# Low parts of the up projection's weights by an accumulating DMA, in a two-layer decoder trunk in split float32

## The chip, the cores and the metric

The kernel runs on one core of a Trainium2 chip. The metric is device time in microseconds (us) of one execution. Before the change it was 2156.09 us in the median of three runs (2155.92 to 2156.14). The five engines of the core work side by side and wait for each other by semaphores: TensorE (PE; its weight loads are PEld), VectorE (DVE), ScalarE (ACT), GpSimd (POOL) and SyncE (SP). In this kernel SP does nothing but issue DMAs.

## The reference

The program is a trunk of two pre-norm residual layers over 1024 tokens of width 1024. The first layer mixes tokens by a convolution and an mLSTM, the second by gated linear attention; behind each mixer stands a SwiGLU feed-forward block of hidden width 2816, and a norm closes the trunk. What the change touches is in the feed-forward blocks:

```python
def swiglu(h, w1, w3, w2):
    return (jax.nn.silu(h @ w1) * (h @ w3)) @ w2

for l in range(DEPTH):
    ...
    h = rmsnorm(x, ffn_norm_g[l])
    x = x + swiglu(h, ffn_w1[l], ffn_w3[l], ffn_w2[l])
```

Everything is float32.

## The kernel before, in words

**Split float32.** PE multiplies operands of a rounded type, float32r. To keep float32's precision every operand x is cut into a high part, x rounded, and a low part, x minus the high part. A product is then three matmuls (lines 168 to 170, in `mm3`): low part of the left operand with the high part of the right, high with low, high with high. In `split` (line 141) ScalarE copies x into the high tile, which rounds it, and VectorE subtracts that from x into the low tile. Tiles named `wH` and `wL` hold the two parts of weights, `hH` and `hL` those of activations.

**The up projection** (`ffn_up`) computes h @ w1 and h @ w3 with seven products instead of eight, in Winograd's form: tokens and the depth are halved, hidden columns are halved too, and each step p of 11 takes 128 columns of each half. Its weights come as four tiles of 128 x 1024, a11, a12, a21, a22 (`load`, line 1021), each with w1 and w3 side by side. The seven products of a step are named after their operands: B11 uses a11, B21 a12, T4 a22, and T1 = a21 + a22, T2 = T1 - a11, T3 = a11 - a21, B22 = a12 - T2 use sums that VectorE makes into tiles `S` (`s`, line 1028). For each product `v(x)` makes the high and low tile of its weights, and `prod` runs 24 matmuls: 12 into a PSUM bank of the kind `mm` (for w1), 12 into one of the kind `sm` (for w3). VectorE and ScalarE take the banks' results apart (lines 1075 and 1082, `c` tiles), and a new tile of the result goes to memory.

**Order of steps.** For p = 0 to 4 (`LEAD = 5`) the products B11 and B21 are made first, ten products in a row, while the norm and the operands of the second half of the tokens are still being made. Then the other five products of p = 0 to 4 follow: T2, T3, T1, T4, B22. From p = 5 on all seven of a step come together, B11 and B21 first. There are 7 x 11 = 77 products per layer, 154 in all.

**Buffers.** `wH` and `wL` have three buffers each, shared with the other weights of the program: the parts of a product can be made when the product three before it has ended. The tiles a11 and a12 (`raw` of the stage's pool) have four buffers, a21 and a22 (`raw` of the program's pool) two, `S` three. A buffer is given again when all its readers are done.

**Order on the engines.** A scheduler of the framework places the program's instructions when it is built. It goes by its own estimate of each instruction's time and by priorities (`high_priority`; here `UOFF = 300`, which lets the preparation of weights run ahead), and each engine then executes its list in the order that was fixed so. An instruction that waits holds up everything behind it on its engine; SP and POOL hold their DMAs in the same way. Norms: `rstd_half` squares eight tiles on ScalarE (line 197), adds them on VectorE (199) and sums over partitions with a matmul on PE (202).

In the profile the products of the up projection are the rows of lines 168 to 170 with `wL` and `wH` of 128 x 1024; the lines of `split` show as L141.

Of the kernel before, what the change touches and what calls it, by code (L numbers as in the profile page):

```python
# [11 lines left out]
AF = mybir.ActivationFunctionType  # L12
ALU = mybir.AluOpType
# [60 lines left out]
def trunk_kernel(ctx, tc, xT, cols, gate_b0, ev_vo0, ev_u, ev_cw, ev_out, od_v0, od_u, od_out, gate_w2, fin_row,  # L74
                 w13, w2, out, xsp, rowd, ud, zd, ad, md):
    nc = tc.nc
    PE, ACT, DVE, POOL, SP = nc.tensor, nc.scalar, nc.vector, nc.gpsimd, nc.sync
# [10 lines left out]
    def nm(s):  # L88
        uid[0] += 1
        return f"{s}_{uid[0]}"  # L90
# [48 lines left out]
    def split(dst, src, lo, after=None):  # L139

        ins = ACT.activation(dst[0], src, AF.Copy), lo.tensor_tensor(out=dst[1], in0=src, in1=dst[0], op=ALU.subtract)  # L141
        for i, a in zip(ins, after or ()):
            behind(i, a)
        return ins[1]

    def behind(ins, other):

        tc.add_manual_dep(ins.ins, other.ins.name, mybir.DependencyInfo(mybir.DependencyClass.NoSync, mybir.DependencyReason.DATA))
# [854 lines left out]
    def ffn_up(l, hv, fp):  # L1003
# [10 lines left out]
        def prep(p):  # L1014
            with tc.high_priority(offset=UOFF):
                def load(q):
                    if q < 2:
                        t = fp.tile([P, 1024], F32, tag="raw", name=nm("raw"), bufs=4)
                    else:
                        t = wp.tile([P, 1088], F32, tag="raw", name=nm("raw"), bufs=2)[:, :1024]  # L1020
                    SP.dma_start(t, w13[l, p, q])
                    return t

                a11, a12 = load(0), load(1)

                def s(x, y, op):
                    t = fp.tile([P, 1024], F32, tag="S", name=nm("S"), bufs=3)
                    DVE.tensor_tensor(out=t, in0=x, in1=y, op=op)
                    return t

                def v(x):
                    hi = wp.tile([P, 1088], F32R, tag="wH", name=nm("wH"))[:, :1024]
                    low = wp.tile([P, 1088], F32R, tag="wL", name=nm("wL"))[:, :1024]
                    split((hi, low), x, DVE)
                    return hi, low

                vs = {"B11": lambda: v(a11), "B21": lambda: v(a12), "T4": lambda: v(ss["a22"])}
                ss = {}

                def sums():  # L1040
                    a21, a22 = load(2), load(3)
                    ss["a22"] = a22
                    ss["T1"] = s(a21, a22, ALU.add)
                    ss["T2"] = s(ss["T1"], a11, ALU.subtract)
                    ss["T3"] = s(a11, a21, ALU.subtract)

                def get(name):
                    with tc.high_priority(offset=UOFF):
                        if name in vs:
                            return vs[name]()  # L1050
                        if not ss:
                            sums()
                        if name == "B22":
                            ss["B22"] = s(a12, ss["T2"], ALU.subtract)
                        return v(ss[name])
                return get
# [491 lines left out]
```

## Time and profile before

| What | before |
|---|---|
| median of three runs | 2156.09 us |
| span of the profiled execution, from first to last instruction | 2155.3 us |
| PE busy / its weight loads | 2145.3 / 1823.8 us |
| VectorE busy | 1541.7 us |
| ScalarE busy | 868.6 us |
| GpSimd busy | 22.9 us |
| data moved by DMA | 279.02 MB, mean 129 GB/s |
| first layer's up projection | from 444 us to 864 us of the span |
| second layer's up projection | from 1516 us to 1935 us of the span |

All times of a stage are in us from the start of the span. The profiled execution is one execution; its span lies 0.8 us below the median of the timed runs. "Idle before" in a row is the time for which the engine stood still before an instruction, and the arrow names what ended it. A name without a number stands for all buffers of that kind.

### The profile page before, as it was taken

Reading aid. Unit: us, or ns where it says so; the run is one execution under the profiler, and the core shown is the slowest. Engines: PE = TensorE matmul, PEld = TensorE weight load, DVE = VectorE, ACT = ScalarE, POOL = GpSimd, SP = SyncE. Lnnn points to the kernel's source line nnn. Section 1 sums busy time; section 2 is a strip of 40 time slices with the busy share of each in tenths; the row PEclk is TensorE's granted clock in tenths of the full one; section 3 lists DMA queues with packets and bytes.
Section 4 is the critical chain, followed back from the end, with each engine's and each line's share of the span. In section 5 each row is a group of like instructions: output and inputs, shape, how many; then the busy total and the mean of one; then the engine's idle time right before and its main releaser. Section 6 shows DMA issues by size and latency. Waiting matters only on the chain.

```text
span 2155.3 us, 28752 instructions
## 1 busy us (share of the span) xinstructions
PE 2145.3 (100%) x10750; PEld 1823.8 (85%) x10750; DVE 1541.7 (72%) x2586; ACT 868.6 (40%) x1426; POOL 22.9 (1%) x56
## 2 busy tenths in 40 slices
PE   9999999999999999999999999999999999999998
PEld 8889988888888888888889989888888888888887
DVE  7555788787776666867877746587877766668687
ACT  6302337453222322444564534355522222234554
POOL 0000000000000000000020000000000000000000
PEclk9999999999999999999999999999999999999999
DMA  4233453654432336645321011155544433265344
GB/s 159 89 123 109 141 140 116 213 187 167 166 135 95 106 107 210 203 118 167 109 71 40 21 49 30 40 160 173 193 149 166 137 95 112 97 244 172 97 128 147
DMA packets 138219, 279.02 MB, mean 129 GB/s; under 512 B 22304, under 2 KB 35488, under 8 KB 138080
## 3 DMA queue, kind: packets, MB, share of 16 engines
q1 hardware_dynamic: 137808, 276.92, 39.6%
q8 instruction: 85, 1.39, 0.3%
q14 instruction: 54, 0.44, 0.1%
q10 hardware_dynamic: 272, 0.26, 0.0%
HBM read 210.51 MB, written 66.62 MB: 129 GB/s over the span
## 4 chain that ended last, share of the span: by engine, by line
PE 99%; DVE 1%; DMA 0%; ACT 0%; issue 0%; SPq 0%; DVEq 0%; ACTq 0%
PE mm L168 21%; PE mm L169 21%; PE mm L170 21%; PE sm L170 9%; PE sm L168 9%; PE sm L169 9%; PE sm L405 2%; PE sm L869 1%; PE sm L888 1%; PE sm L887 1%; PE sm L890 1%; PE sm L618 0%; PE sm L842 0%; PE sm L917 0%; PE sm L620 0%; PE sm L585 0%
## 5 line engine op out<-in xcount | busy, mean ns | idle before, releaser
L169 PE MATMUL mm<-hL,wH 128*128 128x512 f32 x1420 | 557.5, 393 | 0.0
L170 PE MATMUL mm<-hH,wH 128*128 128x512 f32 x1420 | 554.7, 391 | 0.0
L168 PE MATMUL mm<-hH,wL 128*128 128x512 f32 x1420 | 520.2, 392 | 1.3 <-DVE wL L162 1.0
L168 PEld LDWEIGHTS mm<-hH,wL 128*128 128x128 f32 x1420 | 267.0, 188 | 57.5 <-ACT hH L332 1.4
L170 PEld LDWEIGHTS mm<-hH,wH 128*128 128x128 f32 x1420 | 267.2, 188 | 55.1 <-issue 0.2
L169 PEld LDWEIGHTS mm<-hL,wH 128*128 128x128 f32 x1420 | 267.1, 188 | 54.8 <-DVE hL L333 0.5
L169 PE MATMUL sm<-hL,wH 128*128 128x512 f32 x616 | 240.1, 390 | 0.0
L170 PE MATMUL sm<-hH,wH 128*128 128x512 f32 x616 | 239.7, 389 | 0.0
L168 PE MATMUL sm<-hH,wL 128*128 128x512 f32 x616 | 209.0, 390 | 0.0
L141 ACT ACTIVATE wH<-S 128x1024 fp32r<-128x1024 f32 x88 | 93.2, 1060 | 212.4 <-PE sm L170 212.3
L141 ACT ACTIVATE wH<-q 128x512 fp32r<-128x512 f32 x143 | 90.4, 632 | 178.5 <-PE mm L170 101.1
L141 DVE TENSOR_TENSOR wL<-q,wH 128x512 fp32r<-128x512 f32 x143 | 98.6, 689 | 72.2 <-ACT wH L141 71.8
L168 PE MATMUL mm<-wH,hL 128*128 128x256 f32 (+2 forms) x512 | 145.3, 287 | 0.6 <-DVE xy L1271 0.6
L169 PE MATMUL mm<-wL,hH 128*128 128x256 f32 (+2 forms) x512 | 145.6, 286 | 0.0
L170 PE MATMUL mm<-wH,hH 128*128 128x256 f32 (+2 forms) x512 | 145.5, 286 | 0.0
L169 PEld LDWEIGHTS sm<-hL,wH 128*128 128x128 f32 x616 | 115.7, 188 | 24.7 <-issue 0.7
L168 PEld LDWEIGHTS sm<-hH,wL 128*128 128x128 f32 x616 | 115.6, 188 | 24.4 <-PE mm L170 0.5
L170 PEld LDWEIGHTS sm<-hH,wH 128*128 128x128 f32 x616 | 115.6, 188 | 24.2 <-issue 0.2
L141 DVE TENSOR_TENSOR wL<-S,wH 128x1024 fp32r<-128x1024 f32 x88 | 107.4, 1221 | 23.9 <-ACT wH L141 23.9
L1075 DVE TENSOR_TENSOR c<-sm,c 128x512 f32<-128x512 f32 x110 | 75.6, 687 | 67.6 <-PE sm L170 67.6
L161 ACT ACTIVATE wH<-raw 128x1024 fp32r<-128x1024 f32 (+2 forms) x77 | 81.4, 1057 | 96.6 <-PE mm L170 66.7
L162 DVE TENSOR_TENSOR wL<-raw,wH 128x1024 fp32r<-128x1024 f32 (+2 forms) x77 | 94.1, 1222 | 35.4 <-ACT wH L161 35.4
(332 smaller groups left out, 3688.3 us busy)
## 6 DMA issues: line engine op xcount, KB each, us to landing
raw<-in_w SPq DMA_DIRECT2D x108, 512.0 KB
mdT<-c SPq DMA_DIRECT2D x88, 256.0 KB
m<-mdT SPq DMA_DIRECT2D x88, 256.0 KB
mdB<-c SPq DMA_DIRECT2D x66, 256.0 KB
q<-in_w SPq DMA_DIRECT2D x60, 256.0 KB
m<-mdB SPq DMA_DIRECT2D x55, 256.0 KB
xsp<-xy SPq DMA_DIRECT2D x48, 256.0 KB
raw<-in_od_u SPq DMA_DIRECT2D x22, 512.0 KB
```

The costliest lines, as they stand in the source:

```text
L141: ins = ACT.activation(dst[0], src, AF.Copy), lo.tensor_tensor(out=dst[1], in0=src, in1=dst[0], op=ALU.subtract)
L161: first = ACT.activation(hi, raw, AF.Copy)
L162: cuts = lo.tensor_tensor(out=low, in0=raw, in1=hi, op=ALU.subtract)
L168: return (PE.matmul(o, lt[1], rt[0], start=start and not on, stop=False, skip_group_check=on), PE.matmul(o, lt[0], rt[1], start=False, sto ...
L169: PE.matmul(o, lt[0], rt[1], start=False, stop=False, skip_group_check=on),
L170: PE.matmul(o, lt[0], rt[0], start=False, stop=stop, skip_group_check=on))
L405: PE.matmul(o, w[:, m * P:(m + 1) * P], raw[:, e, m:m + NT], start=m == 0, stop=m == SH)
L869: PE.matmul(lb[:, j * P:(j + 1) * P], X[:, 2 * j * P:(2 * j + 1) * P], X[:, (2 * j + 1) * P:(2 * j + 2) * P], start=True, stop=True)
L887: PE.matmul(db[:, cc, :], kw[:, cs], v[:, c, :], start=True, stop=True)
L888: PE.matmul(ob[:, cc, :], A[:, cs], v[:, c, :], start=True, stop=st is None)
L890: PE.matmul(ob[:, cc, :], qt[:, cs], st, start=False, stop=True)
L1075: DVE.tensor_tensor(out=out, in0=a, in1=b, op=ALU.add)
```

## The change

The three lines below replace one call of `split` in `v`. ScalarE now writes both tiles from x: the high one as before, and the low one as the negative of the same rounded value. Then an accumulating DMA, issued on GpSimd's queue, reads x and adds it to the low tile, from SBUF to SBUF, so that the tile holds x minus its rounded value as before. The source is a `raw` tile (three of seven products) or an `S` tile (four of seven). VectorE has no part in it any more. All other weights and activations are split as before.

```diff
                 def v(x):
                     hi = wp.tile([P, 1088], F32R, tag="wH", name=nm("wH"))[:, :1024]
                     low = wp.tile([P, 1088], F32R, tag="wL", name=nm("wL"))[:, :1024]
-                    split((hi, low), x, DVE)
+                    ACT.activation(hi, x, AF.Copy)
+                    ACT.activation(low, x, AF.Copy, scale=-1.0)
+                    POOL.dma_start(low, x, accum_op=ALU.add)
                     return hi, low
```

Lines behind the edit are two higher in the changed kernel; its two copies stand on lines 1034 and 1035, its DMA on 1036.

The scheduler places the instructions anew. Three places show how.

First, TensorE at the start of the first layer's up projection. `wL_760` and `wH_759` are the weights of B11 of p = 0, `wL_771` and `wH_770` those of B11 of p = 1; L202 is the norm's sum for the second half of the tokens. Before:

```order
L168 MATMUL mm_757_4326<-hH3_638_3863,wL_760_4329 128x512
L169 MATMUL mm_757_4326<-hL3_639_3864,wH_759_4328 128x512
L170 MATMUL mm_757_4326<-hH3_638_3863,wH_759_4328 128x512
L168 MATMUL mm_768_4398<-hH0_632_3848,wL_771_4401 128x512
L169 MATMUL mm_768_4398<-hL0_633_3849,wH_770_4400 128x512
```

And with the change:

```order
L168 MATMUL mm_757_4326<-hH3_638_3863,wL_760_4329 128x512
L169 MATMUL mm_757_4326<-hL3_639_3864,wH_759_4328 128x512
L170 MATMUL mm_757_4326<-hH3_638_3863,wH_759_4328 128x512
L202 MATMUL sm_696_4194<-s_688_4171,ones_d_87 128x512
L168 MATMUL sm_758_4327<-hH0_632_3848,wL_760_4329 128x512
L169 MATMUL sm_758_4327<-hL0_633_3849,wH_759_4328 128x512
```

Before, L202 stood behind 12 more matmuls, those of B11 of p = 1 into its first bank; now it stands directly behind the first 12 of the stage.

Second, TensorE in the row of ten products, where the weights of B11 of p = 3 (`wL_793`) take the buffer of those of B21 of p = 1 (`wL_775`). The rows are with the change; left out are 11 more of the same product, `wL_786` (B21 of p = 2).

```order
L168 MATMUL sm_769_4401<-hH7_646_3883,wL_775_4438 128x512
L169 MATMUL sm_769_4401<-hL7_647_3884,wH_774_4437 128x512
L170 MATMUL sm_769_4401<-hH7_646_3883,wH_774_4437 128x512
L170 MATMUL sm_780_4475<-hH3_638_3863,wH_781_4476 128x512
L168 MATMUL mm_779_4474<-hH4_640_3868,wL_786_4512 128x512
...
L168 MATMUL mm_790_4548<-hH0_632_3848,wL_793_4551 128x512
L168 MATMUL sm_791_4549<-hH0_632_3848,wL_793_4551 128x512
```

Between the last matmul that reads `wL_775` and the first that reads `wL_793` stand 13 matmuls; before, it was 36. By the same count 19 matmuls stand between the weights of B11 of p = 2 and the last on the buffer that they take, and 24 for B11 of p = 4.

Third, ScalarE in the regular part, around T2, T3 and T1 of p = 1 (tiles `wH_854`, `wH_858`, `wH_864`) and T4 of p = 1 (`wL_871`), whose source is a22. Before:

```order
L1130 ACTIVATE c_833_4796<-c_833_4796 128x512
L141 ACTIVATE wH_854_4902<-S_852_4898 128x1024
L1134 ACTIVATE c_827_4762<-c_827_4762 128x512
L141 ACTIVATE wH_858_4934<-S_853_4900 128x1024
L1138 ACTIVATE c_812_4686<-c_812_4686 128x512
L141 ACTIVATE wH_864_4968<-S_851_4896 128x1024
```

And with the change:

```order
L1132 ACTIVATE c_833_4809<-c_833_4809 128x512
L1035 ACTIVATE wL_855_4918<-S_852_4913 128x1024
L1034 ACTIVATE wH_854_4917<-S_852_4913 128x1024
L1136 ACTIVATE c_827_4774<-c_827_4774 128x512
L1035 ACTIVATE wL_859_4951<-S_853_4915 128x1024
L1034 ACTIVATE wH_858_4950<-S_853_4915 128x1024
L1140 ACTIVATE c_812_4696<-c_812_4696 128x512
L1035 ACTIVATE wL_865_4986<-S_851_4911 128x1024
L1034 ACTIVATE wH_864_4985<-S_851_4911 128x1024
L1035 ACTIVATE wL_871_5024<-raw_850_4909 128x1024
```

Of each pair the scheduler puts the copy for the low tile first, so that the DMA can be issued while the high tile is copied. On GpSimd the 77 DMAs of a layer stand in the order of the products, each behind a wait for its low tile's copy.

## The prediction

> **What bounds the kernel now.** First the page's top, its DMA queues and its chain of work:
>
> ```profile
> span 2155.3 us, 28752 instructions
> PE 2145.3 (100%) x10750; PEld 1823.8 (85%) x10750; DVE 1541.7 (72%) x2586; ACT 868.6 (40%) x1426; POOL 22.9 (1%) x56
> q1 hardware_dynamic: 137808, 276.92, 39.6%
> PE 99%; DVE 1%; DMA 0%; ACT 0%; issue 0%; SPq 0%; DVEq 0%; ACTq 0%
> ```
>
> TensorE idles 10 us of 2155.3; VectorE is on 1% of the chain. Then the busy times of the stretches in which the two up projections run:
>
> ```profile
> 435.00:500.00 65.00, 65.00 (x286) 53.37 (x285) 52.77 (x72) 33.79 (x51) 0.00 (x0) 1.00 0.56 187
> 500.00:640.00 140.00, 140.00 (x620) 115.95 (x619) 106.31 (x130) 37.13 (x42) 0.00 (x0) 1.00 0.44 151
> 640.00:865.00 225.00, 225.00 (x994) 186.38 (x993) 145.12 (x175) 65.07 (x80) 0.00 (x0) 1.00 0.40 134
> 1507.00:1570.00 63.00, 63.00 (x277) 51.68 (x276) 52.60 (x72) 33.76 (x50) 0.00 (x0) 1.00 0.57 191
> 1710.00:1935.00 225.00, 225.00 (x994) 186.38 (x993) 146.08 (x176) 65.05 (x80) 0.00 (x0) 1.00 0.39 131
> ```
>
> The columns after the stretch are its length, then busy time of PE, PEld, DVE, ACT, POOL, granted clock, DMA share and GB/s. PE is busy for every microsecond of these stretches, at the full clock: 140/620 = 0.226 us per matmul, so a product of 24 matmuls takes 5.42 us. The edited code has nothing to win here; it can only make PE wait.
>
> **What is removed and added.**
>
> ```profile
> L141 DVE TENSOR_TENSOR wL<-S,wH 128x1024 fp32r<-128x1024 f32 x44 | 53.7, 1220 | 11.9 <-ACT wH L141 11.9
> L141 DVE TENSOR_TENSOR wL<-raw,wH 128x1024 fp32r<-128x1024 f32 x33 | 40.2, 1219 | 2.5 <-ACT wH L141 2.5
> L141 ACT ACTIVATE wH<-S 128x1024 fp32r<-128x1024 f32 x44 | 46.6, 1059 | 105.9 <-PE sm L170 105.9
> ```
>
> These groups are those of the first layer's up projection; both layers have 154 low parts. VectorE loses 2 x (53.7 + 40.2) = 188 us, all under a busy PE: worth nothing. ScalarE gains 154 x 1.06 = 163 us; in 500 to 640 it worked 37 of 140 us, so the 26 further copies (28 us) fit. GpSimd gains 154 transfers of 512 KB; it has no other work in these stretches (POOL 0.00).
>
> What changes is when a low part is ready. Its buffer comes free when the product three before it ends; then come the copy on ScalarE and, in place of one subtraction, a time **L** from the end of that copy until PE knows the accumulation landed. The copy of wH runs beside it and is no part of L.
>
> **The price of L.** No accumulating or GpSimd transfer stands in the trace. The nearest row is the 512 KB load of this stage, from its issue on SP to the sum that waits for it:
>
> ```profile
> 507.45 0.33 SPq L1021 DMA_DIRECT2D raw<-in_w  x1
> 511.42 1.23 DVE L1028 TENSOR_TENSOR S<-raw,raw 128x1024 f32<-128x1024 f32 x1 [2.95 <-DMA raw<-in_w]
> 534.71 0.33 SPq L1021 DMA_DIRECT2D raw<-in_w  x1
> 539.13 1.23 DVE L1028 TENSOR_TENSOR S<-raw,raw 128x1024 f32<-128x1024 f32 x1 [3.47 <-DMA raw<-in_w]
> 0.41 0.10 POOL L1521 MEMSET const-uint8-127<- 128x1 uint8 x1
> 1092.53 2.84 POOL L724 TENSOR_SCALAR_AFFINE_SELECT mft<-mft 128x128 f32<-128x128 f32 x1
> ```
>
> That is 4.0 and 4.4 us, mean 4.2. The accumulation reads two tiles: by the q1 row 276.92 MB took 39.6% of the span, so 0.524 MB takes 1.62 us of all sixteen engines, and I add one such reading. GpSimd's issue lies between its shortest and longest instruction, 0.1 and 2.8; I take 0.8, nearer the short end like SP's 0.33, which adds 0.5. L = 4.2 + 1.6 + 0.5 = 6.3 us. Lowest: 0.33 + 1.62 = 2.0, if only the bytes of one reading count. Highest: 2.8 + 4.1 + 2 x 1.62 = 10.1, with the longest issue and each of two reads and the write paid separately.
>
> [...] I stay with 6.3, because the loads of this stage took over 4 us for one reading.
>
> **Where L is longer than its window.** From the last matmul on the buffer to the copy, and from the copy on, around the T2 product of p = 1 and 2:
>
> ```profile
> 531.82 0.39 PE L170 MATMUL sm<-T2H,wH 128*128 128x512 f32 x1
> 532.30 1.06 ACT L141 ACTIVATE wH<-raw 128x1024 fp32r<-128x1024 f32 x1 [4.37 <-PE sm L170]
> 533.46 1.22 DVE L141 TENSOR_TENSOR wL<-raw,wH 128x1024 fp32r<-128x1024 f32 x1
> 540.27 0.68 DVE L1075 TENSOR_TENSOR c<-sm,c 128x512 f32<-128x512 f32 x1
> 542.01 1.22 DVE L1028 TENSOR_TENSOR S<-S,raw 128x1024 f32<-128x1024 f32 x1
> 553.81 0.39 PE L168 MATMUL mm<-T2H,wL 128*128 128x512 f32 x1
> ```
>
> The copy starts some 0.5 us after the product's last matmul and takes 1.06, so L may be the matmuls in between x 0.226 less 1.6. Two whole products lie between in the regular order: 10.8 - 1.6 = 9.2 us, nothing lost at 6.3. But the order of the changed kernel has closer places:
> - Lead, per layer: low part of B11 of p = 2 with 19 matmuls in between (2.7 us allowed), B11 of p = 3 with 13 (1.3), B11 of p = 4 with 24 (3.8), T2 of p = 0 with 36 (6.5), T1 of p = 0 with 31 (5.4). At 6.3: 3.6 + 5.0 + 2.5 + 0 + 0.9 = 12.0.
> - p = 5 to 10, 12 in all: again T2 with 36 and T1 with 31: 0 + 0.9, times 12 = 10.8.
> - T2 of p = 1 to 4, eight in all: the load of a22 (L1021) waits for the buffer that T4's accumulation of p - 1 reads, and SP's queue stands behind it. From 532.30: copy 1.06, L, load until the sum 4.42, sums 2.96 (1.14 from 539.13 to the add at 540.27, 0.6 for that add, 1.22 for the second sum; the low part between them goes), copy 1.06, L; due at 553.81, 21.51 later. 21.51 - 9.50 = 12.0 for 2L, so L may be 6.0; at 6.3 each loses 0.6, together 4.8.
>
> The stall at a stage's start comes from two moves on PE and ACT:
>
> ```profile
> 444.07 0.39 PE L168 MATMUL mm<-hH,wL 128*128 128x512 f32 x1
> 446.79 0.40 PE L168 MATMUL mm<-hH,wL 128*128 128x512 f32 x1
> 449.55 1.02 PE L202 MATMUL sm<-s,ones_d 128*128 128x512 f32 x2
> 444.32 1.06 ACT L141 ACTIVATE wH<-raw 128x1024 fp32r<-128x1024 f32 x1 [3.85 <-issue]
> 445.29 0.61 ACT L197 ACTIVATE t<-xy 128x512 f32<-128x512 f32 x1
> 446.56 0.69 DVE L199 TENSOR_TENSOR s<-s,t 128x512 f32<-128x512 f32 x1
> ```
>
> The norm's matmul L202 now stands behind one group of 12 instead of two, due at 446.8; ahead of the last square ScalarE makes two copies: 444.32 + 2 x 0.97 + 0.61 + 0.69 = 447.6. With the hand-overs PE waits about 1 us, once per layer, and everything behind L202 with it.
>
> Sum: 2 x (12.0 + 1.0) + 10.8 + 4.8 = 41.6 us on the span of 2155.3. The runs' median lies 0.8 above that span (2156.09), so 2197.7, **2198 us**. In general, with brackets below zero left out: S(L) = 2 x [1 + (L-2.7) + (L-1.3) + (L-3.8) + (L-6.5) + (L-5.4)] + 12 x [(L-6.5) + (L-5.4)] + 16 x (L-6.0). S(4) = 10, S(5) = 16, S(7.5) = 99, S(9) = 174.
>
> **The rivals.** 0.2% (4.3 us) is about what a measurement of this kernel can tell from no change.
> - *Hidden* (not slower): an accumulation that lands within 2.4 us of its copy pays at most B11 of p = 3 and the norm: 2 x (1 + 1.1) = 4.2, and at 2.0 3.4 us, 2159. For it: 1.62 us of bytes, SBUF at both ends. Against: single loads take 4.0. Chance 0.08. A true gain has only the 10 us of PE idle, nearly none of them here: 0.03.
> - *Short* (L of 2.4 to 5): the lead alone pays, 4 to 16 us, 2166 at L = 4. Chance 0.2.
> - *One accumulation per product can't be kept*: the DMA engines are 0.40 to 0.56 busy already, 0.44 over a stage's 430 us. In 5.42 us there is room for 0.56 x 5.42 = 3.0 us. Two passes (3.24) overfill it, and if L grows by queueing to 9 the time is 2155.3 + 0.8 + 174 = 2330. Three passes (4.86) make the stage DMA-bound: 0.44 + 4.86/5.42 = 1.34, a third more of 2 x 430 us, 2448. The same price per product falls due if GpSimd's own issue passes 5.42 us. For it: the shares of DMA. Against: packets of an add may overlap their reads. Chance 0.24.
> - [...] Chance 0.08. [...]
>
> **How the numbers follow.** Likeliest is the forecast's case, L of 5 to 7.5: 0.37, 2172 to 2255. The range holds eight tenths: below it the hidden case and a part of the short one, above it the heavier half of the third: 2162 to 2380. Faster 0.03; within 0.2% 0.08; slower 0.89.
>
> **What would show it.** In the new profile the two stretches get longer and the rest stays; PE idles before L168 with a DMA from the GpSimd queue as releaser, mostly in the first 60 us of each stage and at T1 and T2 later; DVE falls by 188 us, ACT rises by 163. Idle before every product, or a DMA share near 1, would show the third rival. No idle on L168 would prove L wrong. Idle of PE on banks, behind sums that wait for S, would be a cause that I have left out.

## The result and the profile after

The changed kernel takes 2274.95 us in the median of three runs (2272.27 to 2281.43) against 2156.09 (2155.92 to 2156.14) before: a ratio of 1.0557, 95% interval 1.0535 to 1.058. It is 119 us slower; the forecast had 42 us, in a range that ended at 2380.

From the page of the changed kernel, its top and the DMA queue of the accumulations (packets, MB, share of the sixteen engines):

```profile
span 2272.9 us, 29372 instructions
PE 2184.1 (96%) x10750; PEld 1838.8 (81%) x10750; DVE 1365.9 (60%) x2432; ACT 1006.1 (44%) x1580; POOL 154.2 (7%) x210
q0 software_dynamic: 22176, 80.75, 18.6%
```

The span grew by 117.6 us with the same 10750 matmuls. Two parts make this up, and both can be read here: PE's busy time grew by 38.8 us (2145.3 to 2184.1), and its idle time by 78.8 us (10.0 to 88.8). VectorE's busy time fell by 176 us and ScalarE's rose by 138; neither is near its limit. The 154 accumulations are queue q0.

The stretches of the first layer's up projection (length; busy time of PE, PEld, DVE, ACT, POOL; granted clock; DMA share; GB/s):

```profile
435.00:500.00 65.00, 62.32 (x262) 49.70 (x261) 38.74 (x59) 41.61 (x60) 8.53 (x11) 0.97 0.88 231
500.00:640.00 140.00, 122.09 (x504) 98.56 (x504) 59.53 (x79) 50.48 (x57) 18.73 (x22) 0.93 0.85 219
640.00:865.00 225.00, 211.69 (x909) 172.98 (x909) 90.87 (x121) 89.50 (x104) 31.54 (x37) 0.98 0.77 186
```

PE was busy for all of these stretches before. The worst is 500 to 640, steps p = 1 to 4: 504 matmuls instead of 620, 18 us idle, and a granted clock of 0.93. So even the matmuls that run are slower on average.

The waits (engine and line that waited, what ended the wait; then us in total, times, longest):

```profile
PE mm L168 <- DMA wL<-S: 43.7, 17, 5.0
PE mm L168 <- DMA wL<-raw: 29.3, 15, 4.3
ACT c L1132 <- DVE c L1077: 148.9, 20, 9.0
DVE S L1028 <- DMA raw<-in_w: 137.2, 24, 8.0
DVE S L1028 <- DMA wL<-S: 136.3, 22, 15.6
PE sm L202 <- DVE s L199: 0.5, 2, 0.3
```

Nearly all of PE's idle time, 73.0 us, ends with the landing of a low part, in only 32 waits for 154 products. VectorE now waits 137 us for loads of a22 at its sums (56.1 us before), and 136 us more, in 22 waits, for accumulations that read the `S` buffer that the next sum will overwrite.

Where the 32 waits are, in the timeline of PE; in brackets the idle time ahead of the row. The rows are of the first layer: one of the lead, four of p = 1 to 4, and three of p = 5 to 10:

```profile
466.64 0.50 PE L168 MATMUL mm<-hH,wL 128*128 128x512 f32 x1 [2.25 <-DMA wL<-raw]
538.41 0.50 PE L168 MATMUL mm<-T2H,wL 128*128 128x512 f32 x1 [3.65 <-DMA wL<-S]
572.54 0.79 PE L168 MATMUL mm<-T2H,wL 128*128 128x512 f32 x1 [4.99 <-DMA wL<-S]
606.78 0.79 PE L168 MATMUL mm<-T2H,wL 128*128 128x512 f32 x1 [4.67 <-DMA wL<-S]
638.69 0.80 PE L168 MATMUL mm<-T2H,wL 128*128 128x512 f32 x1 [2.38 <-DMA wL<-S]
670.01 0.50 PE L168 MATMUL mm<-hH,wL 128*128 128x512 f32 x1 [2.35 <-DMA wL<-raw]
...
753.83 0.50 PE L168 MATMUL mm<-hH,wL 128*128 128x512 f32 x1 [4.32 <-DMA wL<-raw]
...
903.84 0.47 PE L168 MATMUL mm<-hH,wL 128*128 128x512 f32 x1 [3.95 <-DMA wL<-S]
```

Summed over such rows in both layers, and set against the prediction:

| Place | predicted, us | idle of PE, us |
|---|---|---|
| norm's matmul L202 (last row of the waits above) | 2 | 0.5 |
| lead (466.64; B11 of p = 2 to 4, T2 and T1 of p = 0) | 24 | 8.8 |
| T2 of p = 1 to 4 (538.41 to 638.69 above) | 4.8 | 30.5 |
| B11 of p = 5 to 10 (670.01, 753.83) | 0 | 24.8 |
| others of p = 5 to 10 (mostly T1 of p = 10, 903.84; forecast for T1 alone) | 10.8 | 8.9 |
| start of the down projection behind it | 0 | 4.4 |
| slower matmuls (growth of PE's busy time) | 0 | 38.8 |

The idle rows add up to 78.0 of the 78.8 us.

**The chain that makes T2 late.** SP, GpSimd, VectorE, ScalarE and PE between T4 of p = 1 and T2 of p = 2 in the changed kernel:

```profile
546.79 0.84 POOL L1036 DMA_DIRECT2D wL<-raw  x1 [10.18 <-ACT wL L1035]
552.81 0.33 SPq L1021 DMA_DIRECT2D raw<-in_w  x1
559.47 1.23 DVE L1028 TENSOR_TENSOR S<-raw,raw 128x1024 f32<-128x1024 f32 x1 [7.51 <-DMA raw<-in_w]
562.51 1.06 ACT L1035 ACTIVATE wL<-S 128x1024 fp32r<-128x1024 f32 x1 [0.55 <-DVE S L1028]
563.59 0.81 SPq L1021 DMA_DIRECT2D raw<-in_w  x2
563.93 0.84 POOL L1036 DMA_DIRECT2D wL<-S  x1 [10.85 <-ACT wL L1035]
```

T4's accumulation is issued at 546.79; 6.0 us later SP can issue the load of the next a22 into its buffer; the sum starts 6.7 us after that; the copy is ready at 563.57, the second accumulation is issued at 563.93, and PE can use it at 572.54, 8.6 us later. The chain is 25.8 us long from issue to use. By the prediction's terms it is 20.6: 5.9 for the first landing (6.3 less the 0.4 from a copy's end to the issue) + 4.42 + 2.96 + 1.06 + 6.3. The difference of 5.1 us, about what PE waits for at 572.54, is 2.2 us of the load and 2.7 us of the second landing, which takes 9.0 from the copy's end.

Over all eight such chains, in the mean, the first landing took 6.7 us from the copy's end to SP's issue (6.3 in the prediction), the load 5.3 (4.42), and the second landing 9.1 (6.3). The accumulation of T4 itself landed 5.0 to 8.9 us after its issue, that of T2 8.5 to 9.2 in every case. So the second landing is 2.8 of the 4.2 us by which the chain was longer than forecast.

**The chain that makes B11 late** from p = 5 on, ScalarE's and VectorE's rows ahead of the wait at 670.01:

```profile
652.56 0.33 SPq L1021 DMA_DIRECT2D raw<-in_w  x1
658.79 1.23 DVE L1028 TENSOR_TENSOR S<-raw,raw 128x1024 f32<-128x1024 f32 x1 [6.72 <-DMA raw<-in_w]
659.94 0.68 DVE L1077 TENSOR_TENSOR c<-mm,c 128x512 f32<-128x512 f32 x1
660.65 0.63 ACT L1132 ACTIVATE c<-c 128x512 f32<-128x512 f32 x1 [7.72 <-DVE c L1077]
661.19 1.05 ACT L1035 ACTIVATE wL<-raw 128x1024 fp32r<-128x1024 f32 x1
```

It begins at the same late load of a22. VectorE stands 6.72 us at its sum; behind the sum stands the addition of a product (L1077), behind that ScalarE's SiLU (L1132, idle for 7.72 us), and behind the SiLU the copy for B11, whose source a11 had long been there. The accumulation then takes another 7.2 us.

**The slower matmuls.** The stretch around the wait at 572.54, in three parts:

```profile
563.00:570.20 7.20, 4.55 (x21) 3.42 (x19) 4.35 (x7) 6.12 (x8) 1.95 (x3) 1.00 0.73 194
570.20:577.00 6.80, 4.46 (x11) 3.50 (x12) 1.02 (x1) 0.34 (x1) 0.62 (x1) 0.50 1.07 244
577.00:583.00 6.00, 6.00 (x28) 4.97 (x27) 5.38 (x9) 2.01 (x2) 0.86 (x1) 1.00 0.75 236
```

The clock that the throttle granted falls to 0.50 at 570.2, 2.7 us into the idle time, and comes back at 577.0, 4.5 us after PE has resumed. Two consecutive matmuls of this stretch:

```profile
574.41 0.63 PE L169 MATMUL mm<-T2L,wH 128*128 128x512 f32 x1
574.84 0.63 PE L170 MATMUL mm<-T2H,wH 128*128 128x512 f32 x1
```

They start 0.43 us apart; from 577.0 on, 28 matmuls take 6.00 us, 0.21 us each. The trace of the changed kernel has fifteen such stretches before its end, of 3.4 or 6.8 us each, 61 us together, each beside or right behind idle time of PE of 1.8 us or more (twice in two waits close together). Not every such wait has one: none follows the 2.35 us at 670.01. PE is busy for 54 of the 61 us, and at half speed that costs 27 of the 38.8 us. The first matmul behind a wait, 0.50 us at the full clock where one in a row takes 0.226, adds some 7 us in the 27 places outside these stretches. The clock fell here after 2.7 us of idle time, and beside waits as short as 1.8; why one wait has such a stretch and another not, the traces do not show.

### The profile page after: what moved, and what is told of

Its sections match the earlier page's. It is cut to its first block, busy times and chain, and to the rows that moved or that the text cites. A ratio compares the mean times of both kernels' runs of the same rounds, so it can differ in the third digit from the quotient of the medians.

```text
span 2272.9 us, 29372 instructions
## 1 busy us (share of the span) xinstructions
PE 2184.1 (96%) x10750; PEld 1838.8 (81%) x10750; DVE 1365.9 (60%) x2432; ACT 1006.1 (44%) x1580; POOL 154.2 (7%) x210
## 3 DMA queue, kind: packets, MB, share of 16 engines
q0 software_dynamic: 22176, 80.75, 18.6%
## 4 chain that ended last, share of the span: by engine, by line
PE 63%; issue 22%; DMA 9%; DVE 3%; POOL 2%; ACT 1%; POOLq 0%; SPq 0%; DVEq 0%; ACTq 0%
PE mm L168 14%; PE mm L169 14%; PE mm L170 14%; PE sm L168 5%; PE sm L170 5%; PE sm L169 5%; DMA wL<-S 4%; DMA wL<-raw 3%; POOL wL L1036 2%; PE sm L405 2%; PE sm L869 1%; PE sm L888 1%; PE sm L887 1%; PE sm L890 1%; DMA q<-in_w 1%
## 5 line engine op out<-in xcount | busy, mean ns | idle before, releaser
L168 PE MATMUL mm<-hH,wL 128*128 128x512 f32 x1420 | 527.3, 397 | 43.6 <-DMA wL<-raw 29.3
L169 PE MATMUL mm<-hL,wH 128*128 128x512 f32 x1420 | 563.5, 397 | 1.9 <-DVE hL L141 1.9
L170 PE MATMUL mm<-hH,wH 128*128 128x512 f32 x1420 | 560.5, 395 | 0.0
L168 PEld LDWEIGHTS mm<-hH,wL 128*128 128x128 f32 x1420 | 269.5, 190 | 110.4 <-DMA wL<-raw 36.0
L168 PE MATMUL sm<-hH,wL 128*128 128x512 f32 x616 | 209.4, 391 | 0.3
L1035 ACT ACTIVATE wL<-S 128x1024 fp32r<-128x1024 f32 x88 | 93.0, 1056 | 187.8 <-PE sm L168 183.1
L168 PE MATMUL mm<-wH,hL 128*128 128x256 f32 (+2 forms) x512 | 145.3, 287 | 0.7 <-DVE xy L1273 0.6
L168 PEld LDWEIGHTS sm<-hH,wL 128*128 128x128 f32 x616 | 115.9, 188 | 25.6 <-ACT c L1103 1.1
L1028 DVE TENSOR_TENSOR S<-raw,raw 128x1024 f32<-128x1024 f32 x44 | 53.8, 1223 | 133.6 <-DMA raw<-in_w 131.5
L1077 DVE TENSOR_TENSOR c<-sm,c 128x512 f32<-128x512 f32 x110 | 75.5, 687 | 72.3 <-PE sm L170 70.3
L1028 DVE TENSOR_TENSOR S<-raw,S 128x1024 f32<-128x1024 f32 x22 | 27.0, 1226 | 150.9 <-DMA wL<-S 134.1
```

Of the source, the lines that this page charges most:

```text
L168: return (PE.matmul(o, lt[1], rt[0], start=start and not on, stop=False, skip_group_check=on), PE.matmul(o, lt[0], rt[1], start=False, sto ...
L169: PE.matmul(o, lt[0], rt[1], start=False, stop=False, skip_group_check=on),
L170: PE.matmul(o, lt[0], rt[0], start=False, stop=stop, skip_group_check=on))
L1035: ACT.activation(low, x, AF.Copy, scale=-1.0)
L1077: DVE.tensor_tensor(out=out, in0=a, in1=b, op=ALU.add)
```

## The experiments

All experiments change the changed kernel. Each is timed in three rounds, and the ratio is to the kernel before on the same chip, which had medians of 2156.84, 2156.77, 2156.11 and 2156.40 us in the four groups of runs. Where the edit changes what the scheduler sees, it orders the instructions anew; the run with a plain copy keeps the changed kernel's order on PE in every row.

### What the addition itself costs: a plain copy

```diff
-                    POOL.dma_start(low, x, accum_op=ALU.add)
+                    POOL.dma_start(low, x)
```

> The GpSimd DMA copies x into the low tile instead of adding it (same queue, same waits, same bytes written, the tile is not read; the low parts are x itself, so the result is not the reference's). Theory A (the second reading makes the transfer slow: its 4096-byte packets take 328 ns against 159 ns for a load): issue to landing falls from a median of 6.8 us by 1.3 to 2 us, T2 of p = 1 to 4 loses about 8 instead of 32 us, B11 of p = 5 to 10 about 10 instead of 27, time near 2220 us (2205 to 2240). Rival B (GpSimd's issue and the queueing behind SP's loads set the time, not the addition): issue to landing stays above 6.3 us and the time above 2260 us.

Measured: 2171.27 us (2170.6 to 2173.3), ratio 1.0069 (1.0053 to 1.0085). From its page, queue q0 (packets, MB, share of the sixteen engines); then, from the view of the transfer's own line, the time from issue to landing:

```profile
q0 software_dynamic: 22176, 80.75, 10.5%
DMA to landing us min/median/max: 2.9/3.9/8.5
```

and the latter of the changed kernel:

```profile
DMA to landing us min/median/max: 4.5/6.8/11.1
```

With the same 154 transfers, the same order on PE and the same copies on ScalarE, 104 of the 119 us are gone. The addition takes the DMA engines 18.6% x 2272.9 x 0.524/80.75 = 2.7 us per transfer against 10.5% x 2170.1 x 0.524/80.75 = 1.5 us for the copy, and the median landing goes from 3.9 to 6.8 us. Both theories expected more time to remain, a miss. So what the addition does, longer landings together with busier DMA engines, is most of the loss; this run does not part the two. That a transfer stands in the chain at all costs 14 us.

### The copies alone

```diff
                     ACT.activation(low, x, AF.Copy, scale=-1.0)
-                    POOL.dma_start(low, x, accum_op=ALU.add)
```

> Both copies on ScalarE as in the changed kernel, without the accumulating DMA (the low part stays the negated, rounded copy, so the result isn't the reference's). VectorE loses its 154 subtractions and ScalarE gains 154 copies. Theory A: ScalarE's 163 us are hidden, and so VectorE's 188 us bring nothing: 2155 to 2160. Rival B: ScalarE's copies make its other work late (SiLU, the eviction of B11), which is the 15 us that the run with a plain copy lost: 2165 to 2175.

Measured: 2156.47 us (2155.87 to 2157.37), ratio 0.9999 (0.9989 to 1.0008). ScalarE's 154 further copies are wholly hidden, and the time taken off VectorE is worth nothing, both as the prediction had it. The order on PE is neither that of before nor that of the changed kernel in this run. ScalarE has the same copies in both, though, so the 14 us of the plain copy belong to the DMA and the order that it brings, not to ScalarE.

### Cutting T4's chain

```diff
-                def v(x):
+                def v(x, dma=True):
...
+                    if not dma:
+                        split((hi, low), x, DVE)
+                        return hi, low
...
-                vs = {..., "T4": lambda: v(ss["a22"])}
+                vs = {..., "T4": lambda: v(ss["a22"], False)}
```

> T4's low parts (22 of 154) are subtracted on VectorE again, all others stay with the accumulating DMA. Theory A (chain through a22's buffer): the next load of a22 waits until T4's accumulation has read the buffer, so T2 of p = 1 to 4 (32 us of PE idle in the changed kernel) and B11 of p = 5 to 10 (27 us, ScalarE held behind a SiLU whose sums stand behind the late sum T1) both come from T4. Then both fall to under 8 us together, the clock cuts behind them go too (about 20 us), and the time is near 2195 us (2183 to 2210). Rival B (accumulations are too slow or the DMA engines too full in general): a seventh of the transfers is gone, so a seventh of the 119 us: about 2258 us, and T2 stays the costliest place.

Measured: 2207.91 us (2207.01 to 2209.13), ratio 1.0238 (1.0221 to 1.0254): 67 us of the 119 go with 22 of the 154 transfers, where a share by number would have been 17. The waits of its PE, those of its VectorE at the sums for an accumulation, and its landings:

```profile
PE mm L168 <- DMA wL<-S: 22.9, 11, 4.2
PE mm L168 <- DMA wL<-raw: 8.6, 6, 2.4
DVE S L1028 <- DMA wL<-S: 166.2, 32, 15.0
```

```profile
DMA to landing us min/median/max: 4.5/5.9/10.3
```

T2 of p = 1 to 4 waits less, and B11 of p = 6 to 10 no longer at all (it kept 2.4 and 1.4 us at p = 5). That is the evidence that B11's lateness in the changed kernel comes down the chain from T4's landing, through VectorE and ScalarE, and not from its own transfer. The median landing fell too, from 6.8 to 5.9 us, with one transfer in seven gone; but B11's from p = 5 on still took 6.4 us in the median (7.2 before this edit), and in the run below without T3's and T4's transfers 7.1 us, with no wait of PE there.

### The clock: filler matmuls

```diff
+            for _ in range(fill):
+                h = hv["B11", 0][0]
+                ins = PE.matmul(banks[0], h[:, :P], h, start=True, stop=True)
...
-            b = prod(it, "T2")
+            b = prod(it, "T2", None, 10 if 0 < p < LEAD else 0)
```

The ten matmuls (2.3 us) write into the bank that T2's product then overwrites.

> Ten matmuls of 128x512 on old operands, 2.3 us, stand ahead of T2 of p = 1 to 4 on PE, into the bank that T2 then overwrites; they run in the wait for T2's low part (2.6 to 5.2 us each). Theory A (an idle PE has its clock halved for the next one or two windows of 3.4 us): the clock stays full behind these eight waits and the time falls by about 13 us to 2262 us, with T2's landing where it was. Rival B (the clock cuts have another cause, or the slow matmuls are not on the path): 2275 us, within 4 us.

Measured: 2264.87 us (2264.77 to 2270.2), ratio 1.0509 (1.049 to 1.0528) against 1.0557 (1.0535 to 1.058): 10 us faster with 80 matmuls more. The stretch of p = 1 to 4:

```profile
500.00:640.00 140.00, 133.38 (x575) 108.39 (x575) 63.83 (x85) 51.05 (x57) 18.74 (x22) 0.99 0.87 225
```

The granted clock is 0.99 instead of 0.93. The gain lies in the matmuls: PE's busy time less some 19 us of fillers is 2173 us, 11 less than in the changed kernel. It does not lie in the wait: T2's landing got some 1 us shorter in six of the eight places, yet fillers and waits ahead of T2 together take 32.7 us, where the waits took 30.5. The halved clock is therefore a real part of the loss, not only a mark beside it; the fillers reach only T2 of p = 1 to 4, and halved stretches remain elsewhere.

### The order of the loads beside T2's accumulation

Two loads are issued together with T2's accumulation (563.59, x2, and 563.93 above), as soon as T3's sum has freed their buffers; the expectation below takes them for those of a11 and a12. Here the loads of a11 and a12 of p = 1 to 4 go to GpSimd's own queue:

```diff
-                    SP.dma_start(t, w13[l, p, q])
+                    (POOL if q < 2 and 1 <= p < LEAD else SP).dma_start(t, w13[l, p, q])
```

> The loads of a11 and a12 of p = 1 to 4 are issued on GpSimd's queue, where in the regular part they stand behind T2's accumulation, instead of on SP's, where they are issued 0.3 us ahead of it. Theory A (T2's accumulation lands 9 us after its copy because it shares the engines with these two loads): its issue to landing falls to 6.5 us or less, T2 of p = 1 to 4 loses about 12 instead of 32 us, time near 2248 us (2238 to 2258). Rival B (the load of DMA is the same whatever the order): landing and time as before, 2270 to 2280 us.

Measured: 2298.31 us (2293.87 to 2302.16), ratio 1.0656 (1.0639 to 1.0673). A miss: the theory expected a gain and the run lost 23 us more. T2 of p = 1 to 4 still waited about 4 us (2.8 to 5.1 us in the first layer, 2.3 to 3.9 in the second), and the lead got worse, since loads now stood between accumulations on one queue.

The edit did less beside T2 than it was meant to. The two loads there are those of a21, which stayed on SP just ahead of the accumulation, and of a11; a12's comes some 13 us later, behind B22's sum. And a11's moved at p = 1 and 2 alone, to 0.5 to 0.7 us behind the accumulation. At these four places T2's landing took 7.2 to 8.0 us instead of 8.5 to 8.7; at p = 3 and 4, with the second load still within 0.5 us, it took 8.7 to 8.8. So the run does not show that the order of issue is without effect; its loss comes from the lead and not from T2.

### Shorter pieces

```diff
+                    for i in range(2):
-                    POOL.dma_start(low, x, accum_op=ALU.add)
+                        POOL.dma_start(low[:, i * 512:i * 512 + 512], x[:, i * 512:i * 512 + 512], accum_op=ALU.add)
```

> The accumulation in two DMAs of 512 columns each; the first twelve matmuls of a product read the first half only, and the second half is due 12 matmuls (2.7 us) later. Theory A (the landing time L sets the loss): the first half's smaller packets land some 1.3 us earlier, and by the slope between the run with a plain copy (3.9 us, +15 us) and the changed kernel (6.8 us, +119 us), 36 us per us of landing, the places with no chain before them gain, and the a22 chain, which needs both halves, doesn't: 2250, between 2225 and 2270. Rival B (the fixed part of a DMA on this queue, its 0.85 us of issue and its start, outweighs the bytes, and there are 308 of them now): 2275 to 2310.

Measured: 2272.8 us (2265.27 to 2277.16), ratio 1.0533 (1.0508 to 1.0557): no change that can be told from the whole transfers, and a miss for both theories, which had expected a gain or a loss. Landing of the halves:

```profile
DMA to landing us min/median/max: 3.3/6.2/12.2
```

The shortest landing fell by 1.2 us as expected, the median by only 0.6, and GpSimd issues twice per product. T2 of p = 1 to 4 kept waits of 3.1 to 4.1 us in seven of eight places. PE's waits for low parts made from `raw` fell from 29.3 to 9.9 us, those for parts made from `S` rose from 43.7 to 56.3.

### Parts of the change: which products use the DMA

The remaining runs keep the change for some products and make the other low parts on VectorE, by the `dma` argument above; for T3 and B22:

```diff
-                vs = {"B11": lambda: v(a11), "B21": lambda: v(a12), "T4": lambda: v(ss["a22"])}
+                vs = {"B11": lambda: v(a11, False), "B21": lambda: v(a12, False), "T4": lambda: v(ss["a22"], False)}
...
-                        return v(ss[name])
+                        return v(ss[name], name in ("T3", "B22"))
```

The others differ in the names alone. First, two sets of 44, T3 with B22 and T2 with T4:

> Accumulating DMAs only for T3 and B22 (44 of 154); the other low parts by VectorE as before. Theory A (the loss arises only where the time from ScalarE's copy to the landing is longer than the window of that place; two whole products, 9.2 us, lie in the window of T3 and B22, and transfers landed in a median of 5.9 to 6.8 us): nothing lost, 2156 to 2161, PE idle ahead of the low parts under 3 us. Rival B (each accumulating DMA costs by itself, by its load on the DMA engines and on SBUF; 118 us for 154 is 0.77 us each): 2157 + 44 x 0.77 = 2190.

> Accumulating DMAs only for T2 and T4 (44 of 154, as many as in the run with T3 and B22). Theory A (T4's landing holds the buffer of a22, whose load, sums, copy and second landing make T2 of p = 1 to 4 late; from p = 5 the same late sum holds VectorE's queue): with landings of some 5.9 us, a little shorter than in the changed kernel, eight T2 products lose some 2 us each, B11 of p = 5 to 10 some 1 us, and the halved clock after such waits a few us: 2185, between 2170 and 2205, with idle of PE ahead of T2. Rival B (by count): 2190, but then the run with T3 and B22 must show the same time. Rival C (T2 and T4 lose only because the other 110 transfers crowd the queue): 2157 to 2162.

then one product alone, and all but T3 and T4:

> Accumulating DMAs only for B22 (22 of 154). The run with T3 and B22 lost 12 us where nothing was expected; its trace has VectorE wait 4.97 us at B22's sum (S L1028) for T3's landing, since that sum takes the buffer of T3's sum. Theory A (that wait at the head of VectorE's queue is the loss, not the accumulations as such): without T3's transfer nothing is lost, 2155 to 2159. Rival B (each accumulation costs, 12/44 = 0.28 us): 2163.

> Accumulating DMAs only for T3 (22 of 154). Theory A (B22's sum waits on VectorE for T3's landing, and what stands behind it, T4's low part and with it the load of the next a22, is late): the whole loss of the run with T3 and B22, 2164 to 2170. Rival B (by count): 2163. Rival C (the wait on VectorE is hidden, the loss came from B22): 2155 to 2159. A and B are told apart by the run with B22 alone.

> Accumulating DMAs only for T4 (22 of 154). Theory A (the chain from T4's landing over the load of a22 to T2 has room for one landing of some 5 us, not for a second one at its end, as in the run with T2 and T4, +17 us; so neither transfer costs anything alone, as with T3 and B22): 2155 to 2159. Rival B (T4's hold on the buffer of a22 costs by itself, since the load must start later): 2163 to 2170.

> T3's and T4's low parts on VectorE again, the other 110 by accumulating DMA. Theory A (the two transfers whose source buffer is next in turn, T4's raw buffer and T3's sum, make most of the loss; what is left is the lead, some 5 us per layer, T1 and T2 in single places and the cut clock after them; landings fall to some 5.5 us): 2185, between 2172 and 2200. Rival B (by count, 118 x 110/154 = 84): 2241; rival C (T3's wait adds nothing in this company, as with T4 alone on VectorE): 2200 to 2208.

| Low parts by DMA | transfers | landing, min / median | time, us | over before, us | ratio, 95% interval |
|---|---|---|---|---|---|
| T3 | 22 | 4.5 / 4.5 | 2156.42 | 0.3 | 0.9993 to 1.0012 |
| B22 | 22 | 4.5 / 4.7 | 2157.19 | 1.1 | 0.9995 to 1.0014 |
| T4 | 22 | 4.5 / 4.7 | 2158.56 | 2.2 | 1.0 to 1.0019 |
| T3 and B22 | 44 | 4.5 / 4.8 | 2169.11 | 12.3 | 1.0044 to 1.0074 |
| T2 and T4 | 44 | 4.5 / 4.8 | 2173.07 | 16.3 | 1.0052 to 1.0086 |
| all but T3 and T4 | 110 | 4.5 / 5.1 | 2174.72 | 18.6 | 1.0068 to 1.0101 |
| all but T4 | 132 | 4.5 / 5.9 | 2207.91 | 51.1 | 1.0221 to 1.0254 |
| all | 154 | 4.5 / 6.8 | 2274.95 | 118.9 | 1.0535 to 1.058 |

The time by no means follows the number of transfers: 22 cost at most 2 us, at the edge of what a measurement can tell, 44 cost 12 to 16 us, 110 cost 19, and the last 44 cost 100. Both the windows and the landing times are behind this.

The table also shows a second costly product beside T4. Taking T3's 22 transfers out as well, from all but T4 to all but T3 and T4, wins another 33 us, within what was expected of that run. Its accumulation holds the `S` buffer that B22's sum overwrites: VectorE's waits at its sums for accumulations fall from 166.2 us, shown above, to

```profile
DVE S L1028 <- DMA wL<-S: 29.4, 18, 2.8
```

and no wait of PE is left at T2 of p = 1 to 4. T3's transfers alone cost nothing; taken out second they are worth half as much as T4's.

*T3 and B22* was a miss: no loss was expected, since 9.2 us lie in their windows. The trace shows a chain that I had not counted: T3's accumulation reads an `S` tile, and B22's sum, next on VectorE, overwrites that tile. I then expected that wait alone to be the cause, and T3 alone to lose all of the 12 us. It lost nothing, although its trace has the same wait (T3 alone, one step):

```profile
610.77 1.23 DVE L1028 TENSOR_TENSOR S<-raw,S 128x1024 f32<-128x1024 f32 x1 [4.47 <-DMA wL<-S]
619.43 0.33 SPq L1021 DMA_DIRECT2D raw<-in_w  x1
623.47 1.22 DVE L1028 TENSOR_TENSOR S<-raw,raw 128x1024 f32<-128x1024 f32 x1 [3.47 <-DMA raw<-in_w]
```

and with T3 and B22, in the same step:

```profile
616.71 1.22 DVE L1028 TENSOR_TENSOR S<-raw,S 128x1024 f32<-128x1024 f32 x1 [4.97 <-DMA wL<-S]
623.39 0.85 POOL L1039 DMA_DIRECT2D wL<-S  x1 [10.83 <-ACT wL L1038]
625.35 0.74 SPq L1021 DMA_DIRECT2D raw<-in_w  x1
632.53 1.23 DVE L1028 TENSOR_TENSOR S<-raw,raw 128x1024 f32<-128x1024 f32 x1 [6.61 <-DMA raw<-in_w]
636.15 0.50 PE L168 MATMUL mm<-hH,wL 128*128 128x512 f32 x1 [2.88 <-DVE c L1080]
```

Alone, T3's landing is absorbed: the load of a22 at 619.43 is at the sum after 4.0 us. With B22's accumulation issued 2 us ahead of it, the load takes 7.2 us, the sums come late, and PE waits 2.88 us behind VectorE's additions. So the transfers lengthen each other's and the loads' times, and this chain absorbs one of them but not both. T4 looks alike: alone it costs 2.2 us, within what was expected, and with T2 behind it 16; T2 alone was not run. With T2 and T4 eight waits of PE for low parts are left:

```profile
PE mm L168 <- DMA wL<-S: 10.7, 8, 2.6
```

They are the eight T2 products of p = 1 to 4, the place that the prediction had named; B11 from p = 5 on lost nothing there, against my expectation of some 1 us each.

Of all kernels with an accumulating DMA none beats the kernel before; T3 or B22 alone equals it. PE has only 10 us of idle time to win.

## Why the prediction was right and wrong

**Right.** PE is the bound, VectorE's 188 us and ScalarE's 163 us (their busy times moved by 176 and 138) are worth nothing (0.9999 with the copies alone), the change can only make PE wait, and it waits at L168 for a DMA of GpSimd's queue at some places, not before every product. GpSimd's issue was taken as 0.8 us and is 0.85. The fourth rival, with its chance of 0.08, needed issues some 1.2 us longer, and no run shows them: the longest issue of an accumulation took 0.996 us in the changed kernel and 1.24 us in any run (that with loads on GpSimd's queue). The window of T2 of p = 1 to 4, set by the chain over a22's buffer, was the right chain.

**Wrong: one value of L for all places.** The step "L = 4.2 + 1.6 + 0.5 = 6.3 us" is not far off for the whole kernel, in whose median a landing takes 6.8 us from the issue, 7.2 from the copy's end. But it isn't one number. By stretch of the changed kernel, from issue to landing (435 to 500, 500 to 640, 640 to 865):

```profile
DMA to landing us min/median/max: 4.5/5.6/10.2
DMA to landing us min/median/max: 4.8/8.2/9.2
DMA to landing us min/median/max: 4.5/6.0/9.1
```

Some 0.4 us from the copy's end to the issue come on top. For T2 of p = 1 to 4 the prediction had "2L" with 6.3 for both, and a loss of 0.6 us each; 3.8 us each were measured, 30.5 instead of 4.8 in all. The term that failed there is the second L: T2's own landing took 9.1 us from the copy's end. The first one, T4's, was nearly right with 6.7, and the load, taken from before as 4.42, took 5.3. The accumulations make the loads late, and the late load returns in the next low part. The shortest landing, 4.5 us, isn't the time that counts in this kernel. The third rival's mechanism, L growing with the load on the DMA engines, was at work in part (6.8 us with 154 transfers, 4.8 with 44), without its end: the DMA share was 0.77 to 0.88 in the three stretches and most products waited for nothing. The prediction's highest L counts a load as 4.1 us where it had measured 4.0 and 4.4; nothing hangs on that.

**Wrong: a term left out, B11 of p = 5 to 10.** The prediction looked at B11's own window there and found nothing lost. It lost 24.8 us, because the late sum holds VectorE, this the SiLU, and this ScalarE's copy for B11. "Idle of PE on banks, behind sums that wait for S" was named as the sign of a cause left out; what came was a neighbouring path through the same sums, over ScalarE. In the run with T3 and B22 it came just so: five waits, 8.4 us, for VectorE's additions.

**Wrong: a term left out, the clock.** The sum counted matmuls at 0.226 us each, whatever PE had waited before. Waits cost 38.8 us again in slower matmuls, half as much as the idle time itself. By the halved stretches 27 of these come from the granted clock; that they can be bought back by filler work the run with fillers shows for T2 (10 us).

**Wrong in the other direction: the lead and the norm.** The windows of "2.7, 1.3 and 3.8 us" for B11 of p = 2, 3 and 4 were counted as if a low buffer came free at a product's last matmul and as if the buffers went round in turn. The low tile's last reader is the last L168, two matmuls before the end, so the 13 matmuls behind `wL_775` are 15. And B11 of p = 3 got another buffer than I had counted: its copy begins at 473.57 in the first layer, 2 us before the last L168 of B21 of p = 1 (475.64). Of its 5.0 us a layer less than 0.2 was lost. The norm's matmul lost at most 0.3 us where 1 us was predicted. 9.3 us were measured where 26 were forecast, so the first 60 us of a stage, which the prediction named first, were not where PE idled most.

Without these two errors the miss would have been larger still: the places that were forecast too high hid part of what was forecast too low. It is luck as well that the 10.8 us for T1 of p = 5 to 10 come near the 8.9 measured there: the forecast had 0.9 us in each of 12 places, and T1 of p = 10 alone took 7.8 in two.

**Open.** Why an accumulation takes 8 us in one place and 4.5 in another was only narrowed down. The number of accumulations in the program is not all of it: the median of 500 to 640 is 8.2, 7.1 and 5.3 us with 154, 132 and 110 of them, but 6.3 with the 44 of T2 and T4; T2's own at p = 1 to 4 is 8.7, 6.9 and 5.9, but 7.7 with these 44. The traces point at the two loads issued beside T2. With the second load within 0.4 us it lands in 8.5 to 9.2 us (changed kernel); with that load 1.4 to 1.8 us behind, in 7.1 to 7.9 (six places of the run with fillers). Without T3's and T1's accumulations in flight it still takes 7.1 to 8.0 when both loads are some 1 us ahead (T2 and T4), and 5.0 to 5.6 when both are 1 us or more behind (four places of all but T3 and T4). No run moved both loads and nothing else, so this is a reading of traces and not a test. A third buffer for a21 and a22, which would cut T4's chain at its root, wasn't tried.

## What to carry to other kernels

Before a step of 1.2 us on an engine that isn't the bound is replaced by a DMA, follow its source tile as well as its result. In this kernel the next load of a22 was issued 6.0 us after T4's accumulation of p = 1, which reads the buffer, and VectorE waited 136 us at its sums for accumulations that read `S`: a load, a sum or another engine's queue can stand behind that buffer. Price the landing not by a single transfer but in the stretch where it is used, with the loads that are issued beside it there (8.2 us in the median of 500 to 640, where the shortest took 4.8), and expect two landings in one chain to cost where one alone costs nothing (T3 and B22: 12.3 us together, 0.3 and 1.1 alone). The waits of a few us on TensorE cost more than themselves in this kernel: the slower matmuls added half as much again, 38.8 us to 78.8 us of idle time.

## What the runs showed of the hardware

- An accumulating DMA from SBUF to SBUF of 512 KB takes the sixteen DMA engines 2.7 us, a plain copy of the same tiles 1.5 us; it lands in 4.5 us at least and 6.8 in the median of the changed kernel, the copy in 2.9 and 3.9.
- GpSimd's issue of one such DMA took 0.85 us, that of a plain copy about 0.53 (104.8 - 22.9 us of GpSimd's busy time for 154).
- The landing differed by place: 8.5 to 9.2 us for T2 of p = 1 to 4 in the changed kernel, with two loads of 512 KB within 0.4 us of it, and 4.5 us for T3 alone in the median.
- The granted clock fell to half after 2.7 us of idle time and stayed there for 4.5 us behind the wait shown, with matmuls of 512 columns 0.43 us apart.
